# Two small pads at the start of two SBUF pools of a two-block transformer kernel

## The chip, the cores and the metric

The kernel runs on one core of a Trainium2 chip. The metric is device time in microseconds of one execution. Before the change three runs took 3421.7, 3423.7 and 3428.94 us; the median is 3423.7 us.

## The reference, cut to what matters

The input is a residual x of 256 tokens by 2048 channels in float32. It goes through two layers of a first block (windowed attention with a sink, a convolution module and a gated delta rule, side by side), then two layers of a second block (differential attention, gated linear attention and retention side by side, followed by a gated feed-forward part with a short convolution), and a last norm. What costs the time is the same everywhere: a norm of x, a product with a wide weight, some mixing, and a product back to 2048 channels:

```python
for l in range(DEPTH):                    # first block
    h = rms_norm(x, norm_w[l]);  p = h @ w_in[l]
    ...                                   # oa, ob, oc from the columns of p
    x = x + jnp.concatenate([oa, ob, oc], -1) @ w_out[l]
for l in range(DEPTH):                    # second block, in outline
    x = x + mixer(rmsnorm(x) @ w_in_2[l]) @ w_o_2[l]
    x = x + gated(conv(rmsnorm(x) @ w_up_2[l])) @ w_down_2[l]
```

## The kernel before, in words

All of x stays on the chip, transposed: 128 channels on the partitions, 256 tokens along them. A float32 product is made of three products in TensorE's float32r type: each operand is split in a rounded part (hi) and the rest (lo), and hi·hi, hi·lo and lo·hi are summed in PSUM.

The weights come in by DMA from SyncE's queue, 256 rows by 512 columns at a time, into `wr` [128, 2, 512]. ScalarE copies them to `wh` (line 247), VectorE subtracts to get `wl` (line 248). There are four buffers each of `wr`, `wh` and `wl`, in the pool `wp`. The activations that are multiplied with w_in and w_up are `hh` and `hl`, four buffers of each in the pool `hp`, written by the norm (lines 285 and 288). The mixers' outputs `yh`, `yl` are in four units of 512 channels each: the first two units of the first block, and units 0 and 2 of the second, take buffers of `hp`; the others lie in the phase's own pool. The feed-forward activations `ah`, `al` lie in the phase's pool.

The inner loop of nearly all products is lines 370 to 372 (`proj_t_unit`). The weight's 128 x 128 piece is the stationary operand, 256 tokens of an activation are the moving one:

```python
nc.tensor.matmul(o, h[:, kk, cs], hi[:, k], ...)   # L370: wh stationary, hh / yh / ah moving
nc.tensor.matmul(o, h[:, kk, cs], lo[:, k], ...)   # L371: wh stationary, hl / yl / al moving
nc.tensor.matmul(o, l[:, kk, cs], hi[:, k], ...)   # L372: wl stationary, hh / yh / ah moving
```

A unit (512 rows of a weight by 512 columns) is 48 of these. Some products (tile `pn`, lines 422 to 424, `proj_unit`) go the other way round: `hh` or `hl` is stationary, and up to 512 columns of `wh` or `wl` are moving. Between the units the generators of the attention and the other mixers put in their own small steps. The order of the instructions of each engine is fixed when the program is built.

The pools are laid out one behind the other along each partition of SBUF: first `cp` (constants), then `hp`, `wp`, `sp`, then the phase's pool. Before the change the code that opens them is

```python
self.cp = ctx.enter_context(tc.tile_pool(name="cp", bufs=1))
self.hp = ctx.enter_context(tc.tile_pool(name="hp", bufs=4))
self.wp = ctx.enter_context(tc.tile_pool(name="wp", bufs=3))
```

Within an operand, the pieces that one matmul reads start at multiples of 512 bytes from the start of its tile (1024 bytes for each k of an activation, 512 for each 128 columns of a weight). So the place of a tile modulo 512 bytes is the place of all its pieces.

Of the kernel before, what the change touches and what calls it, by code (L numbers as in the profile page):

```python
# [30 lines left out]
# column offsets of the two input projections  # L31
# [7 lines left out]
NSA = 2         # PSUM banks that go round in the attention; as many do in the other mixers  # L39
# [13 lines left out]
def _constants():  # L53
    """Arrays that depend on shapes alone."""
# [17 lines left out]
    # sums of the gates between a position and the middle of its block, level by level  # L72
# [34 lines left out]
def _layout(I):  # L107
    """The inputs, laid out for the kernel: vectors by channel as columns, small ones side by side."""
# [20 lines left out]
def _output(o):  # L129
    """[4, 128, 4, 256] -> [1, 256, 2048]."""  # L130
    return np.ascontiguousarray(o.transpose(0, 2, 1, 3).reshape(D, T).T[None])


class _Kernel:
    def __init__(self, ctx, tc, A):
        self.ctx, self.tc, self.nc, self.A = ctx, tc, tc.nc, A
        self.bg, self.ph, self.final = [], None, False
        self.cp = ctx.enter_context(tc.tile_pool(name="cp", bufs=1))
        self.hp = ctx.enter_context(tc.tile_pool(name="hp", bufs=4))
        self.wp = ctx.enter_context(tc.tile_pool(name="wp", bufs=3))  # L140
        self.sp = ctx.enter_context(tc.tile_pool(name="sp", bufs=2))
# [37 lines left out]
    def tt(self, tag, shape, name, dt=F32):  # L179
        """A tile of the phase's pool; the tag's size and count are in self.tags."""  # L180
        return self.ph.tile(list(shape), dt, tag=tag, name=name, bufs=self.tags[tag])
# [15 lines left out]
    def rsqrt_cols(self, v, src, scale, eps, name, eng=None):  # L197
        """v = (src * scale + eps) ** -0.5 on a few columns: a guess from the bits, three Newton steps."""
# [15 lines left out]
    def sumsq(self, ps, os_):  # L214
        """Sums of squares over the partitions of each [128, 2, 256], as columns: ps[:, 4 i + 2 j + block]."""
        nc = self.nc
        for i, o in enumerate(os_):
            sq = self.t2([P, 2, T], "sq")
            nc.scalar.activation(sq, o, AF.Square)
            for j in range(2):  # L220
                for b in range(2):
                    u = 4 * i + 2 * j + b
                    nc.tensor.matmul(ps[:, u:u + 1], sq[:, j, b * P:(b + 1) * P], self.ones[:, 0:1],
                                     start=True, stop=True)

    def to_rows(self, ps, cols):
        """Each column of cols [128, n] as a row for all partitions: ps [128, n, 128]."""
# [3 lines left out]
    def rows(self, cols, name, n):  # L231
        """Each column of cols [128, n], n up to 32, as a row for all partitions, by way of DRAM: per four of them
        [128, 4, 4, 32] (a quarter of the row, column, 32)."""
# [16 lines left out]
    def softlog(self, x, n, name):  # L250
        """log1p(exp(-|x|)) on a few columns."""
# [19 lines left out]
    def norm_unit(self, i, g):  # L271
        """512 channels of the residual: times the norm's weight, split; their squares' sum by token."""
# [30 lines left out]
    def sum_unit(self, g, eng):  # L303
        """Adds the squares of 512 channels to self.ss [128, 256]."""
# [12 lines left out]
    def norm_rs(self, sums):  # L317
        """1/rms by token."""
# [11 lines left out]
    def wunit(self, W, r0, cols, x=None):  # L330
        """512 rows of a weight, split in two float32r parts: per pair of k tiles (hi, lo).
        With x(), k tile by k tile, each after x(k)."""
# [21 lines left out]
    def proj_t_unit(self, ps, W, r0, cols, x, first, last, done=None):  # L354
        """One unit (hi, lo) of (x W[:, cols])^T -> PSUM [128, tiles, 256], or a list of [128, 512], a bank for each
        tile. With done(), tile by tile, each followed by done(tile)."""
# [28 lines left out]
    def proj_t(self, W, cols, xs=None):  # L385
        """(x W[:, cols])^T -> PSUM [128, tiles, 256]."""
# [6 lines left out]
    def proj_packed(self, W, c0, n):  # L393
        """(x W[:, c0:c0 + n])^T as two sums, of W's hi part and of its lo part -> PSUM [2 n, 256]; n up to 32."""
# [15 lines left out]
    def proj_unit(self, ps, W, cols, x, first, last):  # L410
        """One unit (hi, lo, first row) of x W[:, cols] -> PSUM [128 tokens, 2, 512]."""
# [21 lines left out]
    def load_x(self, new):  # L433
        """The residual, transposed, from DRAM: a tile of 512 channels each."""
# [4 lines left out]
    def begin(self, new, i, W, cols):  # L439
        """Loads x and norms it for the first stage, along with the first units of its weight."""  # L440
# [27 lines left out]
    def add_x(self, W, xs, mid=None, follow=None):  # L468
        """x += y W; with mid(), called when the first two groups of columns have come halfway. follow(g) is called
        when 512 channels of x are done and, but for the last, when a unit of y has been used up."""  # L470
# [38 lines left out]
    def evac(self, ps, n, dst):  # L509
        """PSUM [128 tokens, 2, n] times 1/rms."""  # L510
# [4 lines left out]
    def gate(self, W, c0, n, name, tag):  # L515
        """2 silu of a projection, transposed."""
# [10 lines left out]
    def put_y(self, kt, src):  # L527
        """src [128, 2, 256]: the k tiles kt and kt + 1 of the mixers' output."""
# [13 lines left out]
    def block1(self, l, follow):  # L542
# [32 lines left out]
        # gated delta rule: projections, causal convolution, silu; the keys first  # L575
# [54 lines left out]
    def conv(self, u, c, half, bw, pc, o_bb):  # L630
        """The module's gate and causal convolution, for 256 channels; a generator."""
# [20 lines left out]
    def conv_norm(self, convs, c, pc, offs):  # L652
        """The module's layer norm and silu, split; a generator."""
# [4 lines left out]
        # layer norm over the 512 channels  # L658
# [39 lines left out]
    def ckey(self, t):  # L698
        """Column tile t of the 18 of q, k and v."""
        c, q = self.ct[t]  # L700
        return c[:, q]

    def delta_params(self):
        """Decays and betas by token: [128, chunk, head]."""
# [19 lines left out]
        ef = self.sml([P, 12], "cef")       # exp(cumulated) of chunk 1, exp(rest of the chunk) of chunk 0  # L724
# [9 lines left out]
    def delta_rs(self, t0, scale, name):  # L734
        """1/norms of q or k by token: [128, head, chunk]."""
# [6 lines left out]
        # the keys and queries are twice theirs, and the queries' scale is the root of 1/128  # L742
# [3 lines left out]
    def delta(self):  # L746
        """The gated delta rule in two chunks of 128 tokens, by pairs of heads; a generator."""
# [7 lines left out]
        for p in range(3):  # L755
            yield
            # decay between tokens, transposed: exp of the sum of g over j < t <= i
# [24 lines left out]
        for p in range(3):  # L782
# [5 lines left out]
            # normed keys times minus beta  # L788
# [10 lines left out]
            # its diagonal blocks of 16, by way of DRAM, with a block on each partition  # L799
# [4 lines left out]
        # the blocks of (I + diag(beta) M)^-1, row by row  # L804
# [20 lines left out]
        # then by doubling  # L825
# [33 lines left out]
        # the outputs, still without their queries' factors, over their rms  # L859
# [16 lines left out]
    def blocks(self, t, p):  # L876
        """A pair's part of a DRAM tile [12, 129, 128]: its 32 diagonal blocks of 16, or the matrices by row."""
# [4 lines left out]
    def delta_pair(self, p, q, k, v, g, hb, ef, nbe, xt, intra):  # L882
# [9 lines left out]
        # by token: beta v, and k of chunk 0 with the decay to the chunk's end  # L892
# [11 lines left out]
        # the queries of chunk 1 times exp(cumulated)  # L904
# [7 lines left out]
        # chunk 0, the state after it, chunk 1  # L912
# [35 lines left out]
    def attention_tables(self):  # L948
        """Sines and cosines of the positions: [128 tokens, 2, 8] each."""
# [10 lines left out]
        self.tab = self.cp.tile([P, 2, 2, 8], F32, name="tab")      # [sin | cos]  # L960
# [22 lines left out]
    def attention_in(self, l, W):  # L983
        nc, A = self.nc, self.A
        # norm weights: by row for the rotated part, by column for the rest
# [4 lines left out]
        # rotation tables with the norm weights: cos [c w1 | c w2], sin [-s w2 | s w1]  # L990
        tb = self.sml([P, 2, 2, 2, 16], "atb")       # [token block, q or k, cos or sin, 16]
# [15 lines left out]
        # with the values come the decays and betas of the delta rule  # L1007
# [5 lines left out]
    def attention(self):  # L1013
# [23 lines left out]
        # transposed: heads in pairs on the partitions, each key head on both halves  # L1037
# [19 lines left out]
        # scores, softmax with the sink, values  # L1057
        self.ao = qT            # the outputs take the place of their queries
# [47 lines left out]
    def block2(self, l, load, follow):  # L1106
# [9 lines left out]
        # the gains, with 1 - lambda_init or the half of 2 silu  # L1116
# [4 lines left out]
        # gated linear attention  # L1121
# [18 lines left out]
        # differential attention, by halves of its heads  # L1140
# [9 lines left out]
        # retention  # L1150
# [26 lines left out]
    def values(self, W, c0, name):  # L1177
        """512 columns of values, by token."""
# [5 lines left out]
    def norm_heads(self, os_, kt):  # L1184
        """o over its rms by head, times the gain, in place; a generator."""
# [18 lines left out]
    def gla(self, ga, gw):  # L1204
        """Gated linear attention, both directions, in two blocks of 128 tokens; a generator."""
# [26 lines left out]
        # the products that cross the middle: q and k with their decays, [128, block, head pair, 128]  # L1232
# [3 lines left out]
        for b in range(2):  # L1236
            eqs, eks = [], []
            bs = slice(b * P, (b + 1) * P)
            for pp in range(2):
# [4 lines left out]
                for dst, far, mf, mb, n in ((eq, cq, gm[0], gm[1], 1024), (ek, ck, gm[2], gm[3], 896)):  # L1244
                    yield
                    for c0 in (0, 512):
                        w = min(512, n - c0)
                        px = self.sm(name="gx")
                        # the last level's sums stay in the block: forward in one, backward in the other
# [26 lines left out]
            for lev in range(-1, 7):  # L1276
                yield
                for hh in range(2):          # the halves of the partitions: a bank each
# [40 lines left out]
    def diff_bias(self, new):  # L1319
        """The bias by relative position, in DRAM: [8, 511]; a generator."""  # L1320
# [12 lines left out]
        # each head's row 128 times over: read with rows one element shorter, it is the bias by query and key  # L1333
# [3 lines left out]
    def diff_lambda(self, lam_init):  # L1337
        """Minus the layer's lambda, on all partitions."""
# [13 lines left out]
    def diff(self, half, q, k, v, nlam):  # L1352
        """Four heads of the differential attention; a generator."""
        nc = self.nc
        for h in range(4):
# [7 lines left out]
            for m in range(2):  # L1363
                ps = self.sa([P, 2, T], "dsp")
                d = slice(64 * m, 64 * m + 64)
                for b in range(2):
                    # the bias comes with the second block of queries first
# [35 lines left out]
    def ret_decays(self):  # L1403
        """log of the decays, forward and backward: [128, 8]."""
# [6 lines left out]
    def ret(self, lg, qk, v):  # L1411
        """Retention, both directions; a generator."""
# [192 lines left out]
```

## Time and profile before

| what | value |
|---|---|
| three runs | 3421.7, 3423.7, 3428.94 us |
| span of the profiled execution | 3425.9 us (the page gives no other time for it; it lies within the three runs, 2.2 us over their median) |
| TensorE matmul (PE) | 3367.1 us, 98% of the span, 26498 instructions |
| TensorE weight load (PEld) | 3251.1 us, 95% |
| VectorE (DVE) | 2179.8 us, 64% |
| ScalarE (ACT) | 1635.0 us, 48% |
| GpSimd (POOL) | 261.5 us, 8% |
| DMA | 602.64 MB, mean 176 GB/s |
| mean granted TensorE clock | 0.990 |

The matmuls are pipelined: one lasts some 280 ns by the profile, but the next begins long before that. What tells the time of a stream of them is the spacing, the length of a stretch divided by the number of matmuls that began in it. Such a count over a stretch includes two or three that began before it and were still running.

### The profile page before, as it was taken

The page shows a single profiled execution, that of the slowest core. Times are in us where ns is not written, and L with a number is a line of the kernel's source. Part 1 is how long each engine was busy: PE and PEld are TensorE (multiplying, and loading weights), DVE is VectorE, ACT ScalarE, POOL GpSimd, SP SyncE. Part 2 cuts the span into 40 slices and gives each one's busy share as a digit, 9 for nine tenths or more (in the row PEclk, how much of TensorE's full clock was granted, in tenths as well). Part 3 has the DMA queues.
Part 4 walks back from the last instruction along what each step waited for, and adds up shares of the span by engine and source line. Part 5 has one row for each costly group of instructions (what it writes and reads, how often), then busy time and mean ns, then how long its engine had stood idle before and what let it go on. Part 6 is the DMA issues. An engine that isn't in the chain of part 4 may idle for free. (4 is left out here: it accounts for less than half of the span.)

```text
span 3425.9 us, 63948 instructions
## 1 busy us (share of the span) xinstructions
PE 3367.1 (98%) x26498; PEld 3251.1 (95%) x26498; DVE 2179.8 (64%) x3183; ACT 1635.0 (48%) x2202; POOL 261.5 (8%) x477
## 2 busy tenths in 40 slices
PE   8999989999999999999999999999999999999998
PEld 8899989899998988999999999999889999999998
DVE  8876558886655557666654666555575666546664
ACT  5545444554445445455443445454454545434453
POOL 1210010210010010100000000100101000000000
PEclk9999999999999999999999999999999999999999
DMA  7554476553566554566666666655555666666664
GB/s 216 152 169 125 164 201 189 152 170 103 191 216 198 157 165 148 182 182 185 184 190 192 181 186 187 192 177 155 164 151 178 181 185 184 189 194 183 182 187 151
DMA packets 351652, 602.64 MB, mean 176 GB/s; under 512 B 35314, under 2 KB 92154, under 8 KB 351360
## 3 DMA queue, kind: packets, MB, share of 16 engines
q1 hardware_dynamic: 346800, 585.15, 57.1%
q0 software_dynamic: 4560, 13.40, 1.4%
q8 instruction: 207, 3.39, 0.4%
q14 instruction: 85, 0.70, 0.1%
HBM read 589.40 MB, written 11.15 MB: 175 GB/s over the span
## 5 line engine op out<-in xcount | busy, mean ns | idle before, releaser
L248 DVE TENSOR_TENSOR wl<-wr,wh 128x1024 fp32r<-128x1024 f32 (+2 forms) x1094 | 1309.9, 1200 | 918.9 <-ACT wh L247 910.4
L247 ACT ACTIVATE wh<-wr 128x1024 fp32r<-128x1024 f32 (+2 forms) x1096 | 1127.9, 1031 | 1506.4 <-PE pt L371 1212.9
L370 PE MATMUL pt<-hh,wh 128*128 128x256 f32 x5184 | 1480.3, 286 | 8.0 <-ACT wh L247 8.0
L372 PE MATMUL pt<-hh,wl 128*128 128x256 f32 x5184 | 1479.8, 285 | 3.8 <-DVE wl L248 3.8
L371 PE MATMUL pt<-hl,wh 128*128 128x256 f32 x5184 | 1475.3, 285 | 0.0
L370 PEld LDWEIGHTS pt<-hh,wh 128*128 128x128 f32 x5184 | 997.8, 192 | 20.9 <-ACT wh L247 9.4
L372 PEld LDWEIGHTS pt<-hh,wl 128*128 128x128 f32 x5184 | 997.6, 192 | 9.3 <-DVE wl L248 4.7
L371 PEld LDWEIGHTS pt<-hl,wh 128*128 128x128 f32 x5184 | 998.0, 193 | 4.5 <-issue 4.1
L370 PE MATMUL pt<-ah,wh 128*128 128x256 f32 x1328 | 366.6, 276 | 0.0
L371 PE MATMUL pt<-al,wh 128*128 128x256 f32 x1328 | 366.6, 276 | 0.0
L372 PE MATMUL pt<-ah,wl 128*128 128x256 f32 x1328 | 366.5, 276 | 0.0
L370 PE MATMUL pt<-yh,wh 128*128 128x256 f32 x1024 | 294.9, 288 | 14.6 <-ACT wh L247 8.0
L371 PE MATMUL pt<-yl,wh 128*128 128x256 f32 x1024 | 293.6, 287 | 1.7 <-DVE yl L248 1.7
L372 PE MATMUL pt<-yh,wl 128*128 128x256 f32 x1024 | 292.7, 286 | 0.9 <-DVE wl L248 0.9
L370 PEld LDWEIGHTS pt<-ah,wh 128*128 128x128 f32 x1328 | 249.3, 188 | 0.0
L371 PEld LDWEIGHTS pt<-al,wh 128*128 128x128 f32 x1328 | 249.3, 188 | 0.0
L372 PEld LDWEIGHTS pt<-ah,wl 128*128 128x128 f32 x1328 | 249.3, 188 | 0.0
L370 PEld LDWEIGHTS pt<-yh,wh 128*128 128x128 f32 x1024 | 199.6, 195 | 15.9 <-ACT wh L247 8.9
L371 PEld LDWEIGHTS pt<-yl,wh 128*128 128x128 f32 x1024 | 199.5, 195 | 3.1 <-DVE yl L248 3.1
L372 PEld LDWEIGHTS pt<-yh,wl 128*128 128x128 f32 x1024 | 199.3, 195 | 1.5 <-DVE wl L248 1.5
L423 PE MATMUL pn<-wl,hh 128*128 128x512 f32 (+1 forms) x448 | 169.1, 378 | 1.2 <-DVE wl L248 0.9
L422 PE MATMUL pn<-wh,hh 128*128 128x512 f32 (+1 forms) x448 | 168.9, 378 | 0.0
(585 smaller groups left out, 3086.6 us busy)
## 6 DMA issues: line engine op xcount, KB each, us to landing
wr<-in_w_up_dram SPq DMA_DIRECT2D x352, 512.0 KB, 3.7
wr<-in_w_in_dram SPq DMA_DIRECT2D x320, 512.0 KB, 3.8
wr<-in_w_down_dram SPq DMA_DIRECT2D x176, 512.0 KB, 4.7
wr<-in_w_in_dram SPq DMA_DIRECT2D x158, 256.0 KB, 3.1
wr<-in_w_out_dram SPq DMA_DIRECT2D x64, 512.0 KB, 4.2
wr<-in_w_o_dram SPq DMA_DIRECT2D x64, 512.0 KB, 4.3
xs<-x SPq DMA_DIRECT2D x8, 512.0 KB, 4.3
x<-xs SPq DMA_DIRECT2D x8, 512.0 KB, 8.3
```

The source lines that it names most:

```text
L247: self.nc.scalar.activation(hi, src, AF.Copy)
L248: self.nc.vector.tensor_sub(lo, src, hi.bitcast(F32))
L370: nc.tensor.matmul(o, h[:, kk, cs], hi[:, k], start=start, stop=False, skip_group_check=True)
L371: nc.tensor.matmul(o, h[:, kk, cs], lo[:, k], start=False, stop=False, skip_group_check=True)
L372: nc.tensor.matmul(o, l[:, kk, cs], hi[:, k], start=False, stop=last and k == 3, skip_group_check=True)
L422: nc.tensor.matmul(o, xh[:, k, ts], h[:, kk, :n], start=first and k == 0, stop=False)
L423: nc.tensor.matmul(o, xh[:, k, ts], l[:, kk, :n], start=False, stop=False)
```

## The change

Two tiles that nothing reads or writes are allocated, 32 bytes per partition at the start of `cp` and 64 bytes at the start of `wp`:

```diff
         self.cp = ctx.enter_context(tc.tile_pool(name="cp", bufs=1))
+        self.cp.tile([P, 8], F32, name="pad0")
         self.hp = ctx.enter_context(tc.tile_pool(name="hp", bufs=4))
         self.wp = ctx.enter_context(tc.tile_pool(name="wp", bufs=3))
+        self.wp.tile([P, 16], F32, name="pad1", bufs=1)
         self.sp = ctx.enter_context(tc.tile_pool(name="sp", bufs=2))
```

The rest of the diff takes away comments and docstrings, so line numbers differ. The built program has the same instructions in the same order with the same waits on every engine; only the places of the tiles move, by 32 bytes behind the first pad and by 96 behind the second. In bytes modulo 512, as the built program places them:

| tiles | before | after | weight minus activation, before | after |
|---|---|---|---|---|
| `wr`, `wh`, `wl` | 160 | 256 | | |
| `hh`, `hl`, and `yh`, `yl` in `hp` | 160 | 192 | 0 | 64 |
| `ah`, `al` | 96 | 192 | 64 | 64 |
| `yh`, `yl` of the second block, units 1 and 3 | 480 | 64 | 192 | 192 |
| `yh`, `yl` of the first block, unit 2 | 224 | 320 | -64 | -64 |
| `yh`, `yl` of the first block, unit 3 | 0 | 96 | 160 | 160 |
| identity and ones, in `cp` | 128 | 160 | | |

Before, the places 160, 96, 480 and 224 are all 32 past a multiple of 64; 0 is a multiple. After, 256, 192, 64 and 320 are multiples of 64, and 96 is 32 past one.

## Rows read from the trace of the kernel before

**Rows 1.** The page's first two parts, and the core's span and mean clock.
```profile
PE 3367.1 (98%) x26498; PEld 3251.1 (95%) x26498; DVE 2179.8 (64%) x3183; ACT 1635.0 (48%) x2202; POOL 261.5 (8%) x477
PEclk9999999999999999999999999999999999999999
...
core 0: 3425.9 us, clock 0.990
```

**Rows 2.** Waits: engine, line, waited for: us in total, times, longest.
```profile
PE pt L370 <- ACT wh L247: 16.0, 6, 5.7
PE cum L722 <- POOL cg L716: 9.5, 2, 5.0
PE pt L370 <- ACT yh L247: 6.6, 2, 4.2
PE pt L372 <- DVE wl L248: 4.7, 5, 2.8
PE dpt L1390 <- DVE ds L1387: 3.6, 4, 1.7
...
ACT wh L247 <- PE pt L371: 1212.9, 701, 4.5
```

**Rows 3.** Instruction groups: count | busy us, mean ns of one | idle before.
```profile
L370 PE MATMUL pt<-hh,wh 128*128 128x256 f32 x5184 | 1480.3, 286 | 8.0 <-ACT wh L247 8.0
L370 PE MATMUL pt<-ah,wh 128*128 128x256 f32 x1328 | 366.6, 276 | 0.0
L370 PE MATMUL pt<-yh,wh 128*128 128x256 f32 x1024 | 294.9, 288 | 14.6 <-ACT wh L247 8.0
...
L422 PE MATMUL pn<-wh,hh 128*128 128x512 f32 x384 | 151.0, 394 | 0.0
```

**Rows 4.** Stretches: length, each engine's busy time (instructions), clock, DMA share, GB/s.
```profile
core 0: us, PE busy (x) PEld busy (x) DVE busy (x) ACT busy (x) POOL busy (x), PEclk, DMA share, GB/s
0.00:300.00 300.00, 281.96 (x2009) 264.65 (x2010) 244.23 (x516) 154.54 (x245) 58.38 (x103) 0.96 0.59 171
500.00:800.00 300.00, 294.94 (x2207) 279.58 (x2205) 241.07 (x473) 149.23 (x230) 50.23 (x87) 0.99 0.58 166
1500.00:1700.00 200.00, 200.00 (x1669) 200.00 (x1668) 131.85 (x159) 101.30 (x116) 0.00 (x0) 1.00 0.63 182
1738.69:1869.27 130.58, 130.58 (x1154) 130.58 (x1153) 68.69 (x62) 55.09 (x54) 0.00 (x0) 1.00 0.62 194
447.05:452.81 5.76, 5.76 (x51) 5.76 (x49) 3.68 (x4) 2.12 (x2) 1.65 (x2) 1.00 0.62 202
452.81:458.46 5.65, 5.65 (x50) 5.65 (x49) 4.50 (x7) 4.67 (x7) 1.37 (x2) 1.00 1.03 221
1427.20:1438.51 11.31, 11.31 (x99) 11.31 (x98) 4.91 (x4) 4.24 (x4) 0.00 (x0) 1.00 0.62 189
18.20:21.40 3.20, 3.20 (x16) 3.20 (x16) 3.20 (x3) 3.20 (x8) 3.10 (x3) 0.50 1.08 364
```

**Rows 5.** Timeline of PE: start us, duration us; a product with 512 moving columns.
```profile
1037.63 0.39 PE L422 MATMUL pn<-wh,hh 128*128 128x512 f32 x1
...
1041.72 0.39 PE L422 MATMUL pn<-wh,hh 128*128 128x512 f32 x1
```

**Rows 6.** Timeline of PE at the lower clock, 256 moving columns.
```profile
18.63 0.41 PE L370 MATMUL pt<-hh,wh 128*128 128x256 f32 x1
...
20.55 0.41 PE L370 MATMUL pt<-hh,wh 128*128 128x256 f32 x1
```

**Rows 7.** Chain that ended last, in order of time: float32 matmuls, 256 moving columns.
```profile
2456.26 0.86 PE dpo L1395 x4
```

## The prediction, made before the changed kernel ran

> **What bounds the kernel now.** I read the page's busy shares first, then the waits, then the stretches. [...] The largest waits of TensorE add up to 40 us in 19 waits, while ScalarE waited 1212.9 us until TensorE had released a buffer for the next part of a weight [rows 2]. So weights are ready early, and TensorE's stream of matmuls sets the end. A change pays if it shortens the spacing of that stream, and nothing else in this diff can pay: the instructions, their order and their waits stay.
>
> The reader is to see in the stretches that the spacing is not the same everywhere, though every matmul of lines 370 to 372 has the same shape, type and clock (1.00). In the up product, where the moving `hh` and the stationary `wh` begin at the same place modulo 512, 200 us hold 1669 matmuls less 2 carried in: 120.0 ns. In the down product, where `ah` begins 64 bytes before `wh`, 130.58 us hold 1152: 113.35 ns. A unit of the first block's output product with `yh` at place 0 takes 5.76 us for 48: 120.0 ns; the next, with `yh` at 224, 5.65 us: 117.7 ns; the second block's at 480 take 11.31 us for 96: 117.8 ns [rows 4]. The units at 0 and at 224 follow each other in one product, and the quicker one has the heavier work beside it (DMA share 1.03 against 0.62), so the place, not the stage, is the best single explanation. [...]
>
> [...]
>
> **The change part by part.** The pads cost no instruction. What they do is per matmul.
>
> First, the bulk: line 370 has 5184 matmuls on `hh`, and lines 371 and 372 as many [rows 3], 15,552; of the 3 x 1024 on `yh` and `yl` half (1536) read `hp` buffers too. That is 17,088 at 120.0 ns. [...] After the change the relation is that of `ah`, so 113.35 is the upper end that a row shows. [...] So 16,600 x 11.0 ns = 183 us (ends 110 and 221).
>
> Second, `ah` and `al`: 3 x 1328 = 3984 [rows 3], whose relation stays and whose alignment improves: 113.35 to 109.0, 17 us (ends 0 and 26).
>
> [...]
>
> Fourth, the other 1536 matmuls on `yh` and `yl` keep their distance to the weights; three quarters become aligned, a quarter loses it. Ends 0 and 14 us (all to 109); I take 5.
>
> The identity and the ones move off a multiple of 64. [...] VectorE's, ScalarE's and the DMAs' work moves its places too; with 64%, 48% and waits on TensorE in front of them, a few per cent there stay hidden.
>
> Sum: 183 + 17 + 13 + 5 = 218 us less on TensorE.
>
> What is late next: the waits of TensorE [rows 2] are chains (norms, gates) that run under other matmuls, and matmuls that go 9% faster cover less. If each of 19 waits has some 10 us of cover in front of it, 9% of 190 us is 17 us; ends 0 and 40. VectorE is busy 81% in the first 300 us and 80% between 500 and 800 [rows 4]; 9% faster makes that 88%, close to full in places. In the feed-forward part it is at 66% in the up and 53% in the down product [rows 4], with room. I take 10 us of give-back in all. The DMA share there, 0.63 at 182 GB/s, would go to 0.69.
>
> So 3425.9 - 218 + 10 = 3218 us for the profiled execution, which lies 2.2 us over the median of the runs: 3216, rounded to 3215.
>
> [...]
>
> **The rivals.**
>
> Only the distance matters, alignment does nothing. For it: `ah` at 113.35 is the best float32r spacing in the trace, and `yh` at 0, the only aligned moving operand, is no faster than 120.0. [...] Bulk 110, `pn` 8, nothing else, give-back 6: 3425.9 - 112 - 2.2 = 3312 us.
>
> VectorE becomes the bound in the first block. Its two stretches of 300 us at 80% [rows 4] then keep their length, and 9% of 600 us, less what is already given back, returns some 35 us: 3250 us. For it: the share; against it: waits on `wl` are 4.7 us in all [rows 2], and a share of 88% is not yet 100%.
>
> The change does nothing, since the place is not the cause, and `ah` is quicker because its stage is lighter (VectorE 53% against 66%). Against it stand the neighbouring units at 117.7 and 120.0. Time 3424 us. [...]
>
> Slower: an aligned moving operand is worse, as `yh` at 0 (120.0) against `yh` at 224 (117.7) can be read. Then `hh` stays at 120 and `ah` goes from 113.35 to 120: 3984 x 6.65 = 26 us, 3450 us. It decides where the new spacing exceeds 118.7 ns, at which 16,600 matmuls gain (1.3 ns each) what 3984 lose (5.35 each). Against it: the distance is 160 there and 64 here.
>
> **How the numbers follow.** The forecast (both distance and alignment count, spacing 106.7 to 111) has 0.53, its own range 3150 to 3260. Only the distance 0.29, VectorE 0.07, nothing 0.06, slower 0.05. The range 3145 to 3320 takes in the first three and leaves out 11% for the last two and some 8% for the tails. A change of 0.2%, 7 us, is about what can be told from none. Faster 0.53 + 0.29 + 0.07 = 0.89, same 0.06, slower 0.05.
>
> **What would show it.** In the up product 200 us hold 1835 matmuls at 109.0 (1875 at 106.7, 1764 at 113.35, 1667 if nothing changes). The down product stands at 109.0 as well; if it stays at 113.35 while the up product reaches the same, only the distance counted. `pn` at 215.6. TensorE's waits of some 10 to 20 us more, and `wl` not among the largest of them; if `wl` is, VectorE has become the bound. The forecast is wrong if the up product's spacing stays above 115 ns, or if TensorE's busy share falls under 95%.

## The result, and the profile after

The changed kernel took 3369.48, 3368.74, 3398.29 and 3397.43 us, a median of 3383.45 us against 3422.86 us (four runs) for the kernel before: a ratio of 0.9882 [0.9855, 0.9909]. It is faster, by 39 us where 209 were forecast, and outside the range that the prediction gave. The profiled execution took 3369.48 us with a span of 3367.7 us; before it was 3425.9 us, so the trace has 58.2 us to explain. Lines 370, 371, 372 and 422 of before are 372, 373, 374 and 424 of after.

The page's shares and instruction groups, to be read against [rows 1, 3]; columns as there:

```profile
PE 3308.9 (98%) x26498; PEld 3191.5 (95%) x26498; DVE 2175.3 (65%) x3183; ACT 1636.5 (49%) x2202; POOL 259.8 (8%) x477
...
L372 PE MATMUL pt<-hh,wh 128*128 128x256 f32 x5184 | 1457.8, 281 | 8.3 <-ACT wh L249 8.3
...
L372 PE MATMUL pt<-ah,wh 128*128 128x256 f32 x1328 | 369.6, 278 | 0.0
...
L372 PE MATMUL pt<-yh,wh 128*128 128x256 f32 x1024 | 292.4, 286 | 12.4 <-ACT wh L249 7.7
```

TensorE is busy 58.2 us less (3367.1 to 3308.9), as much as the span lost. The bound is the same engine, and the whole gain is in its stream. The mean duration of one matmul on `hh` falls by 5 ns (286 to 281); that of one on `ah`, which the forecast made quicker, rises by 2.

The largest waits of the after kernel (engine, line, waited for: us in total, times, longest), against [rows 2]:

```profile
PE pt L372 <- ACT wh L249: 16.0, 6, 5.6
PE cum L724 <- POOL cg L718: 10.9, 2, 5.6
PE pt L374 <- DVE wl L250: 4.8, 4, 2.6
PE pt L372 <- ACT yh L249: 4.7, 2, 3.4
PE dpt L1392 <- DVE ds L1389: 3.2, 3, 1.7
```

Together they are 39.6 us, where they were 40.4. Nothing was turned into a new wait.

Stretches of the after kernel, against [rows 4] (length, busy time and instructions of PE, PEld, DVE, ACT, POOL, then clock, DMA share, GB/s). The first two are the stretches in the first block; then come the up products of layers 0 and 1, their down products, and units on `yh` whose distance to the weight (weight's place less activation's, in bytes) is 160, -64 and 192:

```profile
0.00:300.00 300.00, 281.09 (x2058) 263.16 (x2059) 248.09 (x527) 155.72 (x249) 59.07 (x103) 0.97 0.58 175
500.00:800.00 300.00, 294.07 (x2222) 277.32 (x2221) 243.88 (x484) 149.62 (x233) 46.45 (x86) 0.98 0.55 164
1500.00:1700.00 200.00, 200.00 (x1768) 200.00 (x1767) 136.79 (x163) 104.40 (x118) 0.00 (x0) 1.00 0.62 194
2700.00:2900.00 200.00, 200.00 (x1700) 200.00 (x1699) 134.61 (x161) 101.77 (x115) 0.00 (x0) 1.00 0.59 186
1703.39:1833.95 130.56, 130.56 (x1155) 130.56 (x1154) 68.66 (x62) 55.11 (x54) 0.00 (x0) 1.00 0.60 195
2878.11:3013.79 135.68, 135.68 (x1155) 135.68 (x1153) 68.69 (x62) 54.83 (x54) 0.00 (x0) 1.00 0.59 187
440.99:446.73 5.74, 5.74 (x50) 5.74 (x49) 2.45 (x2) 2.12 (x2) 1.11 (x1) 1.00 0.73 159
446.73:452.39 5.66, 5.66 (x51) 5.66 (x49) 4.50 (x7) 4.67 (x7) 1.38 (x2) 1.00 0.92 149
1407.56:1418.87 11.31, 11.31 (x99) 11.31 (x98) 4.91 (x4) 4.24 (x4) 0.00 (x0) 1.00 0.58 196
```

Read the counts (two or three of each are carried in). The same up product, at the same clock of 1.00, with the same tiles at the same places, holds 1766 matmuls in 200 us in layer 0 (113.3 ns each) and 1698 in layer 1 (117.8 ns). The down products go with their layers: 1152 matmuls take 130.56 us (113.3 ns) in layer 0 and 135.68 us (117.8 ns) in layer 1, where `ah` had 113.35 before. So the new distance does not have one spacing; it has two, and each lasts. By the start times, 6184 matmuls of layer 0 follow each other at 113.3 ns (700.85 us), and 6185 of layer 1 at 117.8 ns (728.45 us). That is 27.6 us between two layers with the same work. In the first block and the mixers the spacing changes from unit to unit between the same two values.

The timeline of PE where each layer's lasting stream begins (start us, duration us), around the four small matmuls that write 1/rms to all partitions; layer 0, then layer 1:

```profile
1458.10 0.28 PE L372 MATMUL pt<-hh,wh 128*128 128x256 f32 x1
...
1458.58 0.28 PE L373 MATMUL pt<-hl,wh 128*128 128x256 f32 x1
1458.69 0.61 PE L231 MATMUL bcps<-base,xrs 128*128 128x128 f32 x4
1459.06 0.37 PE L374 MATMUL pt<-hh,wl 128*128 128x256 f32 x1
1459.26 0.28 PE L372 MATMUL pt<-hh,wh 128*128 128x256 f32 x1
...
1459.72 0.28 PE L373 MATMUL pt<-hl,wh 128*128 128x256 f32 x1
...
2623.28 0.28 PE L372 MATMUL pt<-hh,wh 128*128 128x256 f32 x1
...
2623.74 0.28 PE L373 MATMUL pt<-hl,wh 128*128 128x256 f32 x1
2623.85 0.60 PE L231 MATMUL bcps<-base,xrs 128*128 128x128 f32 x4
2624.21 0.36 PE L374 MATMUL pt<-hh,wl 128*128 128x256 f32 x1
2624.41 0.28 PE L372 MATMUL pt<-hh,wh 128*128 128x256 f32 x1
...
2624.89 0.28 PE L373 MATMUL pt<-hl,wh 128*128 128x256 f32 x1
```

The instructions are the same; four spacings then take 0.46 us in the one and 0.48 us in the other, and it stays so to the end of the layer. In the exact times the gap after `bcps` differs by 5 ns (206 and 201). The rows ahead of `bcps` show the reverse: four spacings take 0.48 us ahead of layer 0's quick stream and 0.46 us ahead of layer 1's slow one, 117.8 and 113.4 ns over the last fourteen spacings. In both places the spacing behind the four small matmuls is the other one of the two.

`pn`, 20 spacings of the product with 512 moving columns (the first and the last start):

```profile
1029.66 0.39 PE L424 MATMUL pn<-wh,hh 128*128 128x512 f32 x1
...
1034.24 0.39 PE L426 MATMUL pn<-wh,hl 128*128 128x512 f32 x1
```

4.58 / 20 = 229 ns, against 4.09 / 18 = 227.2 before [rows 5]: no gain. In `pn` the activation is the stationary operand, so there the stationary one lies 64 bytes below the moving one along the partition, and not 64 above it as in the other products.

### The profile page after: what moved, and what is told of

It is laid out like the page before. It is cut to its first block, busy times and chain, and to the rows that moved or that the text cites. A ratio compares the mean times of both kernels' runs of the same rounds, so it can differ in the third digit from the quotient of the medians.

```text
span 3367.7 us, 63948 instructions
## 1 busy us (share of the span) xinstructions
PE 3308.9 (98%) x26498; PEld 3191.5 (95%) x26498; DVE 2175.3 (65%) x3183; ACT 1636.5 (49%) x2202; POOL 259.8 (8%) x477
## 5 line engine op out<-in xcount | busy, mean ns | idle before, releaser
L372 PE MATMUL pt<-hh,wh 128*128 128x256 f32 x5184 | 1457.8, 281 | 8.3 <-ACT wh L249 8.3
L374 PE MATMUL pt<-hh,wl 128*128 128x256 f32 x5184 | 1457.8, 281 | 3.6 <-DVE wl L250 3.6
L373 PE MATMUL pt<-hl,wh 128*128 128x256 f32 x5184 | 1453.0, 280 | 0.0
L372 PEld LDWEIGHTS pt<-hh,wh 128*128 128x128 f32 x5184 | 985.3, 190 | 21.2 <-ACT wh L249 9.6
L374 PEld LDWEIGHTS pt<-hh,wl 128*128 128x128 f32 x5184 | 979.4, 189 | 9.0 <-DVE wl L250 4.4
L373 PEld LDWEIGHTS pt<-hl,wh 128*128 128x128 f32 x5184 | 980.8, 189 | 4.5 <-issue 4.1
L426 PE MATMUL pn<-wh,hl 128*128 128x512 f32 (+1 forms) x448 | 169.4, 378 | 0.0
```

What stands on the lines that cost most here:

```text
L372: nc.tensor.matmul(o, h[:, kk, cs], hi[:, k], start=start, stop=False, skip_group_check=True)
L373: nc.tensor.matmul(o, h[:, kk, cs], lo[:, k], start=False, stop=False, skip_group_check=True)
L374: nc.tensor.matmul(o, l[:, kk, cs], hi[:, k], start=False, stop=last and k == 3, skip_group_check=True)
L426: nc.tensor.matmul(o, xl[:, k, ts], h[:, kk, :n], start=False, stop=last and k == 3)
```

## The experiments

**The second pad alone.** The change has two pads: `pad0` (32 bytes) moves everything behind the constants, `pad1` (64 bytes) puts the weights 64 bytes from the activations. This kernel takes out the first, so that all large operands again begin 32 bytes past a multiple of 64, at a distance of 64:

```diff
-        self.cp.tile([P, 8], F32, name="pad0")
```

> The 64 bytes in the weights' pool alone: hh and hl are 64 bytes before the weights modulo 512 as in the changed kernel, but everything begins 32 bytes past a multiple of 64, as before. Theory A (only the distance modulo 512 counts, and at a distance of 64 the stream of matmuls can run in either of two lasting rhythms, 113.35 or 117.8 ns): the same two rhythms for hh, some hundreds or thousands of matmuls in a row each, none at 120; the time between 3335 and 3400 us. Rival B (the distance alone gives 113.35, as ah had before, and the alignment to 64 spoils it): hh and ah at 113.35 throughout, 3305 to 3320 us. Rival C (the alignment brought the gain): hh at 120, 3424 us.

Measured: 3370.97 us (3369.43 to 3377.93, four runs) against 3425.17 us, ratio 0.9845 [0.9831, 0.9860]. The up products of layers 0 and 1:

```profile
1500.00:1700.00 200.00, 200.00 (x1700) 200.00 (x1699) 134.01 (x160) 100.46 (x116) 0.00 (x0) 1.00 0.65 187
2700.00:2900.00 200.00, 200.00 (x1767) 200.00 (x1766) 138.86 (x168) 106.62 (x122) 0.00 (x0) 1.00 0.66 194
```

The gain of the change is there in full without the alignment, with the same two spacings, and in this execution layer 0 has the slower one.

**The first pad alone.** Operands at multiples of 64, the distance of `hh` to the weights 0 as before:

```diff
-        self.wp.tile([P, 16], F32, name="pad1", bufs=1)
```

> The 32 bytes in the constants' pool alone: hh, hl, the weights' parts, ah and al all begin at multiples of 64; hh stands at the same place as the weights modulo 512 (192), ah 64 bytes before them. Theory A (only the distance counts): hh at 120.0 ns as before, ah at 113.35, the time within 7 us of 3423. Rival C (the alignment to 64 counts): hh under 117 ns, at least 50 us faster. Rival B (alignment spoils): ah in two rhythms, hh at 120 or more, up to 30 us slower.

Measured: 3423.96 us (ten runs), ratio 0.9994 [0.9984, 1.0003]. The up and the down product of layer 0:

```profile
1500.00:1700.00 200.00, 200.00 (x1669) 200.00 (x1668) 132.82 (x160) 102.40 (x117) 0.00 (x0) 1.00 0.64 182
1736.03:1866.61 130.58, 130.58 (x1155) 130.58 (x1154) 68.67 (x62) 55.08 (x54) 0.00 (x0) 1.00 0.63 194
```

These are [rows 4] again, 1669 in 200 us and 1152 in 130.58 us, though both operands are now aligned. Alignment to 64 bytes changes neither: the up product stays at 120.0 ns and the down product at 113.35.

**Which distances are quick.** Two kernels with one feed-forward part and the end alone (the rest of the computation is left out), in which each buffer of `hh`, `hl`, `ah`, `al` is 64 bytes longer, so that each unit of a product stands at another distance. The diff is the first kernel's and leaves out `hl`, `ah` and `al`, which are lengthened like `hh`; the two last pads stand ahead of the first `ah` and the first `al`. The second kernel has `pada` of 16 and `pad1` of 80 columns:

```diff
-        h = self.hp.tile([P, 4, T], F32R, tag="hh", name=f"hh{g}")
+        h = self.hp.tile([P, 4 * T + 16], F32R, tag="hh", name=f"hh{g}")
+        h = h[:, :4 * T].rearrange("p (a b) -> p a b", a=4)
+        self.hp.tile([P, 64], F32, name="padh", bufs=1) if g == 0 else None
...
+                    self.ph.tile([P, 8], F32, name="pada", bufs=1)
+                    self.ph.tile([P, 16], F32, name="padb", bufs=1)
-    def run(self, stages=("b1", "b1", "b2", "f", "b2", "f", "end")):
+    def run(self, stages=("f", "end")):
```

> Only one feed-forward layer is left, without the rest of the network. The four buffers of hh (and of hl) begin at distances of 128, 192, 256 and 320 bytes before the weights modulo 512, the seven of ah (and al) at odd multiples of 32 (32, 160, 224, 288, 352, 416, 480). Each distance then lasts for 48 matmuls at a time. Theory A (a table by distance, no spacing under 113.35): 192 at 117.8; the others somewhere between 113.35 and 120; odd multiples of 32 irregular, near 120 as yh at 160. [...]

> Only one feed-forward layer is left. hh and hl at distances of 64, 0, 448 and 384 before the weights modulo 512, ah and al at 0, 128, 192, 256, 320, 384 and 448. Theory A: 0 at 120.0, 64 at 113.35 or 117.8, 192 and 448 at 117.8, and for each distance the same value with ah as with hh here or in the run beside it, although the tiles lie elsewhere. [...] If the place itself and not the distance counts, ah and hh at one distance differ.

Measured, a single run each: 780.46 and 780.62 us. Four units that follow each other, 48 matmuls each: in the first kernel at distances 320, 128, 192 and 256,

```profile
85.37:90.83 5.46, 5.46 (x50) 5.46 (x49) 5.25 (x10) 4.09 (x6) 0.00 (x0) 1.00 0.66 183
90.83:96.53 5.70, 5.70 (x50) 5.70 (x49) 3.76 (x4) 2.12 (x2) 0.00 (x0) 1.00 0.55 165
96.53:102.19 5.66, 5.66 (x51) 5.66 (x50) 2.45 (x2) 2.12 (x2) 0.00 (x0) 1.00 0.71 214
102.19:107.94 5.75, 5.75 (x50) 5.75 (x49) 2.45 (x2) 2.12 (x2) 0.00 (x0) 1.00 0.62 187
```

and in the second at 64, 384, 448 and 0:

```profile
85.19:90.65 5.46, 5.46 (x50) 5.46 (x49) 5.25 (x10) 4.09 (x6) 0.00 (x0) 1.00 0.67 187
90.65:96.35 5.70, 5.70 (x50) 5.70 (x49) 3.76 (x4) 2.12 (x2) 0.00 (x0) 1.00 0.56 155
96.35:102.01 5.66, 5.66 (x51) 5.66 (x50) 2.45 (x2) 2.12 (x2) 0.00 (x0) 1.00 0.72 222
102.01:107.77 5.76, 5.76 (x51) 5.76 (x50) 2.45 (x2) 2.12 (x2) 0.00 (x0) 1.00 0.66 184
```

The two lists are the same to 0.01 us: in these four units 256 bytes more make no difference. Over the units behind `bcps`, from the start times, without the first few spacings of each:

| distance, and the same plus 256 | ns per matmul |
|---|---|
| 0, 256 | 120.0 |
| 32, 288 | 118.3 |
| 64, 320 | 113.4, or 117.8 |
| 128, 384 | 118.7, and 120.0 in one unit of each (352, that is 96 plus 256: 118.7 and 117.3) |
| 160, 416 | 119.9 |
| 192, 448 | 117.8 |
| 224, 480 | 116.7, and 117.8 in one unit at 480 |

`hh` and `ah` at the same distance have the spacings of one row of the table, as in the changed kernel, where both products stand at 113.3 in layer 0 and at 117.8 in layer 1. So no part of the stage shows in them, and nothing is under 113.3. Whether 64 gives 113.4 or 117.8 goes with what ran just before. All 42 entries from a unit at 0 or 256 (2016 matmuls) gave 113.4, and so did two from units at 384 and 416; the one entry in each kernel behind the small matmuls gave 117.8, for the 43 matmuls to the unit's end. What ran before counts at other distances too: the units with 120.0 at 128 and 384 are those right behind this slow one.

**Setting the spacing, first try.** If the stream's last distance decides, six matmuls at distance 0 behind the small ones should put each layer at 113. They write a bank that nothing reads again (the edits of this try and the next are made to the changed kernel):

```diff
             nc.vector.tensor_copy(self.bc, ps.rearrange("p a b -> p (a b)"))
+            for _ in range(6):
+                nc.tensor.matmul(ps.rearrange("p a b -> p (a b)"), self.hi[0][:, 0, 0:P], self.hi[0][:, 0],
+                                 start=True, stop=True)
```

> The changed kernel with six extra matmuls after each norm's row of 1/rms (five times; nothing reads what they write). Both of their operands are the same tile of hh, so their distance modulo 512 is 0. Theory A (a stretch at distance 64 that is entered from matmuls at distance 0 runs at 113.35 and stays there until other instructions come between): both feed-forward layers at 113.35 from the first to the last matmul behind the six, in every run; the time 3340 to 3350 us, 25 to 60 us less than the changed kernel, and with a spread under 10 us. Rival E (the rhythm is set by what the feed-forward stage does beside TensorE, or at random as it goes): one or both layers at 117.8 still, 3365 to 3400 us.

The control takes the stationary operand from 64 bytes on (`16:16 + P`), so that the six stand at distance 64:

> The same six extra matmuls, but with the stationary operand taken 64 bytes further on, so that their distance is 64 and not 0. Theory A: they keep whatever rhythm they begin in, so that each feed-forward layer may come out at 113.35 or at 117.8; the time within 3340 to 3400 us, by the number of slow layers (27 us each). Rival F (any extra matmuls, or the delay, do what the six at distance 0 do): both layers at 113.35 in every run and the same time as the run beside it within 5 us.

And the changed kernel once more, on the same chip:

> The changed kernel once more, beside the two others on one chip. Theory A: times in steps of about 27 us, by how many of the two feed-forward layers run at 117.8: near 3342, 3369 or 3397 us, and nothing over 3405. Rival E: times spread evenly between these.

Measured: with the six at distance 0, 3403.37 us (six runs, 3394.76 to 3406.27) against 3428.79 us, ratio 0.9924 [0.9911, 0.9936]; the control 3402.88, 3406.11, 3349.1 and 3402.43 us, too far apart for a ratio, three of them over the 3400 that was expected at most; the changed kernel 3401.0 us (six runs: 3370.88, 3381.16, and four from 3400.0 to 3407.34, one of them over the 3405 that was expected at most), ratio 0.9915 [0.9893, 0.9937]. The up products of layers 0 and 1, first with the six at distance 0, then of the changed kernel again:

```profile
1500.00:1700.00 200.00, 200.00 (x1701) 200.00 (x1700) 134.01 (x160) 100.80 (x115) 0.00 (x0) 1.00 0.64 187
2700.00:2900.00 200.00, 200.00 (x1701) 200.00 (x1700) 133.73 (x160) 100.64 (x115) 0.00 (x0) 1.00 0.64 187
```

```profile
1500.00:1700.00 200.00, 200.00 (x1701) 200.00 (x1700) 133.63 (x160) 101.10 (x115) 0.00 (x0) 1.00 0.64 187
2700.00:2900.00 200.00, 200.00 (x1767) 200.00 (x1766) 138.37 (x166) 105.30 (x120) 0.00 (x0) 1.00 0.66 194
```

The expectation fell: both layers stand at 117.8 ns (6162 matmuls each), the wrong one of the two. The profiled control shows 117.8 in both layers as well, but not for the same reason, as the start times around the six show. In the control the spacing behind the six is the one ahead of them in all six places of the kernel: 113.3 in four, 117.8 in the two feed-forward layers. The six at distance 0 gave 117.8 in all six places, from 113.3 in four of them. One of these, in the first block (start us, duration us; four spacings take 0.45 us ahead and 0.47 us behind):

```profile
535.45 0.28 PE L376 MATMUL pt<-hl,wh 128*128 128x256 f32 x1
...
535.90 0.88 PE L305 MATMUL bcps<-hh 128*128 128x256 f32 x6
536.62 0.28 PE L377 MATMUL pt<-hh,wl 128*128 128x256 f32 x1
...
537.09 0.28 PE L375 MATMUL pt<-hh,wh 128*128 128x256 f32 x1
```

The changed kernel is the other way round than in its first profile: 117.8 in layer 0, 113.3 in layer 1, with the same instructions. What decides can be read from the traces. In the six whole-kernel traces with `hh` at 64 (after, second pad alone, and the four runs of the two tries) the four small matmuls `bcps` come 36 times in a stream of `hh`, and each time the spacing behind them is the other one: 117.8 to 113.3 in 29, 113.3 to 117.8 in 7. So a feed-forward layer is slow where the few matmuls on `hh` ahead of `bcps` were quick. This is read from the traces; no run was made to test it. Which spacing those few have differs from execution to execution, and the kernel's times mostly lie in clusters about one layer's 27.6 us apart (3381.16 lies between). The control's 3349.1 us fits both layers at 113; that run was not traced.

**Setting the spacing, second try.** What the entries from 0 or 256 in the two kernels of distances have and the first try has not: there the moving operand changes its place while the stationary one stays; in the first try the stationary one changed. So the six now have both operands at the place of `wh`, and the moving one then steps down 64 bytes to `hh`. They stand before the second column group of each layer's up product, and the next product there starts its sum anew:

```diff
# proj_t_unit, after the weight's unit is made
+        if self.rhythm:
+            self.rhythm = False
+            for _ in range(6):
+                nc.tensor.matmul(ps[:, 0], w[0][0][:, 0, :P], w[0][0][:, 0, :T], start=True, stop=False,
+                                 skip_group_check=True)
# the feed-forward part
+                    self.rhythm = (b, s) == (0, 1)
```

> The changed kernel with six extra matmuls before the second column group of each feed-forward layer's up product (twice in all; nothing reads what they write). Both operands are the same tile of wh, at 256 modulo 512; at the end of the six the moving operand steps 64 bytes down to hh while the stationary one stays where it was. Theory A2 (the step by which the stream comes to distance 64 decides: a step of the moving operand down gives 113.35, as in all 1920 matmuls of the two sweeps that came from 0 or 256 and as hh to ah before; a step of the stationary one up gives 117.8, as in the run with the six on hh): both layers at 113.35 from the six to their end in every run, 3340 to 3352 us, spread under 10 us. Rival F (extra matmuls at distance 0, however placed, lead to 117.8): 3395 to 3407 us. Rival E (at random): layers mixed, 3345 to 3405 us.

Measured: 3349.86 us (five runs, 3342.84 to 3355.18) against 3427.86 us, ratio 0.9770 [0.9747, 0.9792]. The two up products, and PE's timeline at the entry of layer 0 (start us, duration us):

```profile
1500.00:1700.00 200.00, 200.00 (x1767) 200.00 (x1766) 138.66 (x165) 106.64 (x120) 0.00 (x0) 1.00 0.64 195
2700.00:2900.00 200.00, 200.00 (x1767) 200.00 (x1766) 139.49 (x165) 106.16 (x120) 0.00 (x0) 1.00 0.63 194
```

```profile
1468.69 0.28 PE L379 MATMUL pt<-hh,wl 128*128 128x256 f32 x1
...
1469.15 0.87 PE L367 MATMUL pt<-wh 128*128 128x256 f32 x6
1469.85 0.28 PE L377 MATMUL pt<-hh,wh 128*128 128x256 f32 x1
...
1470.21 0.28 PE L377 MATMUL pt<-hh,wh 128*128 128x256 f32 x1
```

From there 6140 matmuls of each layer follow each other at 113.3 ns (695.87 us). The six take 0.7 us per layer. But in this execution both layers were quick already ahead of the six: the first row shows it for layer 0 (four spacings in 0.46 us), and in both layers the last 42 matmuls on `hh` ahead of the six stand at 113.3 to 113.4 ns, `bcps` having followed a stream at 117.8. So the trace shows that the quick spacing holds behind the six, not that they end a slow one. That they bring back the 27.6 us of a slow layer is argued from the 42 entries of the kernels of distances, and from the times: no run has a time that a slow layer would give, while each of the changed kernel's ten has. No changed kernel ran beside this one on the same chip, so a share of chance in where its layers fell is not excluded. Two of the five runs lie above the 3352 us that were expected, and their spread is 12.3 us where under 10 was expected. This version is quicker than the kernel before and than the changed one: its ratio lies below both ratios of the changed kernel, 0.9882 [0.9855, 0.9909] and 0.9915 [0.9893, 0.9937], with the intervals apart, and all its five runs are under all ten of the changed kernel.

## Why the prediction was wrong

**What bounds the kernel: right.** The gain came from the stream's spacing alone. Span and busy time of TensorE fell by the same 58.2 us, and its waits stayed within 1 us in all.

**The step that failed** is that alignment to 64 bytes counts beside the distance. The first pad alone aligns the operands and leaves `hh` at 120.0 and `ah` at 113.35; the second pad alone leaves them 32 bytes past a multiple and has the whole gain (ratio 0.9845). No run shows the 109.0 ns behind the 183, the 17 and the 5 us of the sum, or the 106.7 ns of its ends: at a granted clock of 1.00 the float32r streams with 256 columns stood between 113.3 and 120.0 ns. Nor does a run show the 215.6 ns of `pn` behind the 13 us (1152 matmuls, from 227.2), or what would give the 8 us of the rival: `pn` went from 227.2 to 229 ns. The 109.0 lay below every float32r spacing of the trace. With this step fall the terms for `ah`, for `pn` and for the other `yh`, all of which rested on alignment, and 4.35 ns per matmul of the bulk (109.0 instead of 113.35).

**The part that no rival had** is that a distance of 64 has two spacings. Before, `ah` at 64 showed a mean of 113.35 ns over 4220 spacings, 4208 of them under 115, and gave no hint of the other; it came behind the up product at distance 0, the entry that gave 113.4 in all 42 cases later. After the change the whole feed-forward part stands at 64 and keeps for a layer the spacing that the four small matmuls left.

The terms of the sum, from start times in the two profiled executions:

| term | predicted | measured | why |
|---|---|---|---|
| bulk | -183 | 16,400 x (119.88 - 115.3) = -75 | 113.35 at best, and 117.8 in near half of it |
| `ah`, `al` | -17 | 4222 x (115.55 - 113.35) = +9 | layer 1 went from 113.35 to 117.8 |
| `pn` | -13 | about 1090 x (229.6 - 227.65) = +2 | alignment does not help there, and its stationary operand comes to lie 64 below the moving one, not above it |
| other `yh` | -5 | 0 | 192 and -64: 117.8; 160: 120 as before, aligned or not |
| given back | +10 | +6, what the rows above leave to 58.2 | largest waits -0.8; the mean clock went from 0.990 to 0.988, 0.2%: by estimate some 6 us |

The count of the bulk was right (16,600 forecast, 17,088 less some 3% by the author's estimate; 16,400 found); that of `ah` and `al` left out 240 that write other tiles, worth 1 us. The gain per matmul of the bulk was off in two parts: 4.35 ns for the alignment that does nothing (109.0 against 113.35), 71 us, and 2.0 ns for the slower spacing in a part of it (115.3 against 113.35), 32 us.

**The rivals.** "Only the distance matters" named the right cause and 3312 us. The measured kernel missed it by the second spacing (the last line of the bulk, and `ah`) and the 8 us given to `pn`; the version with the set entry comes to 3349.86. Of these 38 us its bulk explains 14 (16,400 at a mean of 114.2, as units of the first block and the mixers are still slow in part) and `pn` 8 that were not gained; the rest was not taken apart. VectorE did not become the bound: it is busy 248 of 300 us and 244 of 300 in its two full stretches, where it was 244 and 241, and the waits on `wl` went from 4.7 to 4.8 us. "Nothing" and "slower" fell with the ratio, though `ah` did lose in one of the two layers, by the second spacing and not by its alignment.

The first two lines of "what would show it" worked as tests: 200 us of the up product held 1766 in layer 0, as the prediction had named for 113.35, and the down product stayed at 113.3. Its words "only the distance counted" held. The count in layer 1 was none of the four that it named, and its 117.8 ns is over the 115 that was to show the forecast wrong.

## What to carry to other kernels

When the stream of matmuls is the bound, divide stretches of equal length by their counts, product by product and layer by layer: the same instructions at the same clock can hold two spacings 4% apart (113.3 and 117.8 ns here), and a group's mean (281 ns in place of 286) hides it. Before such a difference is called chance, compare what ran ahead of the stream in each case: here 36 of 36 entries behind `bcps` went by it. Where the places of the moving and the stationary operand differ between products, tabulate spacing by distance before a cause is named, and test each half of a two-part change alone; here one half gave everything and the other 0.9994 [0.9984, 1.0003]. A value that lies beyond every row of the profile, as 109.0 did, belongs at the end of the range and not in its middle.

## What the runs showed of the hardware that was not expected

In these kernels the spacing of the float32r matmuls with 256 columns went with the distance of the two operands along the partition, from 113.3 to 120.0 ns at a granted clock of 1.00, and not with their alignment to 64 bytes (the first pad alone: 0.9994). In the two kernels of distances four units whose distances differ by 256 bytes took the same time to 0.01 us. At equal places 256 columns more cost 227.2 - 120.0 = 107.2 ns before [rows 4, 5]; if all columns cost as much, some 13 ns of the 120.0 come beside them. This is an estimate from two products that differ in which operand moves.

At distance 64 the stream showed two lasting rhythms, 113.3 and 117.8 ns; each was kept over more than 6000 matmuls. A step of the moving operand from the stationary one's place gave the first in all entries seen (42 in the kernels of distances, 113.4 ns); a step of the stationary one gave the second in all six, in one kernel (117.8 ns). Six matmuls at distance 64 itself left either rhythm as it was (113.3 in four places, 117.8 in two). The four small matmuls changed either into the other in 36 of 36 cases, with a gap behind them of 206 or 207 ns where 113.3 followed and 201 where 117.8 did.

Open are what the part beside the columns is, why the kinds of entry differ (the claim for the stationary operand rests on the first try alone), what sets the rhythm ahead of the small matmuls in an execution, whether the six of the second try turn a slow layer quick (no trace caught one), the distance 96, and whether the products with 512 columns would gain with the stationary operand 64 bytes above the moving one.
